# Reordering the seven Strassen block products of the FFN's second matrix in a two-layer decoder trunk

## The chip, the cores and the metric

The kernel runs on one core of a Trainium2 chip. The metric is the time of one execution on the device, in microseconds (us), smaller being better. Several executions were timed; one more was run under the hardware profiler, and everything said about engines, waits and transfers comes from that one.

## The reference

The program is a decoder trunk of two layers on 256 tokens of width 1024, all in float32. Each layer is a half-step feed-forward network (FFN), a mixer (a spatial gating branch beside differential attention) and a second half-step FFN, each followed by a residual sum and a layer norm. What the change touches is the second matrix of the FFN, `w2`, which stands four times in the program (two layers, two FFNs each):

```python
def _swiglu(x, w1, w3, w2):
    return (jax.nn.silu(x @ w1) * (x @ w3)) @ w2
...
    for l in range(DEPTH):
        h = _swiglu(x, ffn_w1[l, 0], ffn_w3[l, 0], ffn_w2[l, 0])
        x = _layernorm(ALPHA * x + 0.5 * h, ln_g[l, 0], ln_b[l, 0])
        h = _mixer(x, l, w_in[l], ...)
        x = _layernorm(ALPHA * x + h, ln_g[l, 1], ln_b[l, 1])
        h = _swiglu(x, ffn_w1[l, 1], ffn_w3[l, 1], ffn_w2[l, 1])
        x = _layernorm(ALPHA * x + 0.5 * h, ln_g[l, 2], ln_b[l, 2])
```

With h the 256 x 2816 hidden activation, `h @ w2` has 256 x 1024 outputs: two row tiles of 128 tokens by two column halves of 512.

## The kernel before

**Split operands.** A float32 operand is used as a sum of two parts that TensorE multiplies fast: a high part `whi`, copied by ScalarE (ACT), and a low part `wlo`, the difference, made by VectorE (DVE). A product takes three matmuls: high by high, low by high, high by low. Every weight therefore arrives by DMA as a raw tile, is split by one ACT and one DVE instruction for each piece of 128 x 1024, and is then used by TensorE (PE). `stream` does that for plain weights (its splits are lines 195 and 197), `pieces` for weights that take part in Strassen sums (both parts at lines 247 and 249, in `split`). There are eight buffers for high parts, eight for low parts (`HL`), and four for raw tiles (`RAW`).

**The w2 stage, `gemm_seven`.** The first 1024 of the 2816 rows of w2 are taken as a 2 x 2 block matrix w11, w12, w21, w22 (each 512 x 512), the first 1024 columns of h as a 2 x 2 matrix over the two row tiles, and their product is made by the Strassen-Winograd scheme with seven block products in place of eight. `product` issues one of them: 12 matmuls into one PSUM bank. The remaining rows of w2 are ordinary. For the first column half they come as seven pieces, and `between` takes one piece for both row tiles, which is again 12 matmuls. For the second column half `rest(1)` splits seven more pieces, which are held and used first for one row tile, then for the other (line 402).

So until `rest(1)` begins TensorE works through 14 slots of 12 matmuls, seven block products and seven pieces of `between`. They are counted here as slots 1 to 14. Before the change the order is: slot 1 w11 by block a11; 2 a piece; 3 w21; 4 a piece; 5 the sum r1 = w11 + w12 into the bank `bz`; 6 a piece; 7 the sum r1 + r3 (r3 is w22) into the bank `bx`; 8 a piece; 9 the plain block r3 into `bz`; 10 a piece; 11 r2 = w12 + w22 into `bx`; 12 a piece; 13 the last block product, r1 after w21 was added to it, into `bx`; 14 a piece.

**Sums on the way.** `plus` adds one raw tile to another on VectorE (line 356, two instructions of 128 x 1024). `gather` does the addition w21 into r1 by an accumulating DMA that GpSimd (POOL) issues in two halves (line 350); it may start once the splits of r1 + r3 have read r1. `ln.fold` (line 605, VectorE) adds the running content of `bx` or `bz` into the residual rows `xtok` in SBUF. TensorE goes on accumulating in the same bank, so the next product into that bank must wait until the fold has read it. There are five folds in each stage: after slot 1 (`bx`), after slot 5 (`bz`), after slot 7 (`bx`, the product with `sums[1]`), after slot 11 (`bx`) and after slot 13 (`bx`).

**What sets the order.** TensorE runs strictly in program order (a manual schedule). The other engines' orders are fixed when the program is built: a list scheduler takes what is ready in its own model of time, earlier program positions first, and each engine's queue then runs in that order on the chip. On top of that the `line` mechanism chains the high splits on ACT, and the low splits and `plus` additions on VectorE, in program order, from the start of the FFN's later part to the end of `rest(1)`. Folds are not in that chain, so where a fold stands between the splits is the scheduler's choice. Raw tiles are fetched by SP in one queue in the order of `step`.

**Timed side tasks.** `beside` tasks resume when a clock that `beat` advances by 1 for each 12 matmuls of this kind has gone far enough. `setup`, which runs once in the first FFN, waits 16 beats after its DMAs and then issues a few small VectorE instructions (lines 552 to 566) and one exponential on ACT (line 559).

Of the kernel before, what the change touches and what calls it, by code (L numbers as in the profile page):

```python
# [54 lines left out]
def trunk(ctx, tc, x, xT, w13a, w13b, w2, wb, wqk, wu, wg, wgr, wbr, wbrr, wo, gateb, gatebr, sgug, sgub, sguwT, sgubias, lam, diffg,  # L55
# [18 lines left out]
    def name(s):  # L74
        serial[0] += 1
        return f"{s}_{serial[0]}"

    def bank():
        return psum.tile([P, 512], F32, tag="main", name=name("bank"))

    def side_bank():
        return psum.tile([P, 512], F32, tag="side", name=name("sbank"))
# [18 lines left out]
    def s512(s, n=4):  # L101
        return tmp.tile([P, 512], F32, tag="side", name=name(s), bufs=n)
# [21 lines left out]
    def beat(w):  # L124

        clock[0] += w
        for task in list(tasks):
            if task[0] <= clock[0]:
                turn(task)
# [20 lines left out]
    def inline(eng, ins):  # L150
        if line[2]:
            line[eng is V] = ins
        return ins

    def behind(ins):

        return tc.issue_after(ins) if ins is not None else nullcontext()

    def fetch(src, width=CH, raw=None):

        step()
        if raw is None:
            raw = raw_pool.tile([P, CH], F32, tag="raw", name=name("raw"))
        for g in gate:
            g[0] -= 1
        while len(gate) > 1 and gate[1][0] < 0:
            gate.pop(0)
        with behind(gate[0][1] if gate and gate[0][0] < 0 else None):
            if isinstance(raw, list):
                for j, v in enumerate(raw):  # L170
                    loaded[0] = nc.sync.dma_start(v, src[:, j * HC : (j + 1) * HC]).ins
            else:
                loaded[0] = nc.sync.dma_start(raw[:, :width], src).ins
        return raw
# [70 lines left out]
    def split(hi, lo, src, eng=V, after=(None, None)):  # L245
        with behind(after[0]):
            a = A.activation(hi, src, AF.Copy).ins  # L247
        with behind(after[1]):
            return a, eng.tensor_tensor(out=lo, in0=src, in1=hi.bitcast(F32), op=ALU.subtract).ins  # L249
# [94 lines left out]
    def halved(v):  # L344
        return v if isinstance(v, list) else [v[:, o : o + HC] for o in range(0, CH, HC)]
# [7 lines left out]
    def plus(raw, more):  # L353
        for v, m in zip(halved(raw), halved(more)):
            with behind(line[1]):
                inline(V, V.tensor_tensor(out=v, in0=v, in1=m, op=ALU.add).ins)  # L356
        return raw

    def pieces(raw):
        out = []  # L360
        for v in halved(raw):
            hi = hi_pool.tile([P, HC], F32R, tag="hi", name=name("whi"))
            lo = lo_pool.tile([P, HC], F32R, tag="lo", name=name("wlo"))
            for eng, ins in zip((A, V), split(hi, lo, v, after=line[:2])):
                inline(eng, ins)
            out.append((hi, lo))
        return out

    def product(ps, x, w, start, stop):
        for k in range(4):  # L370
            hi, lo = (v[:, k % 2 * 512 : k % 2 * 512 + 512] for v in w[k // 2])
            for n, (y, o) in enumerate(((hi, 0), (lo, 0), (hi, 1))):
                PE.matmul(ps, x[o](k), y, start=start and k == n == 0, stop=stop and k == 3 and n == 2,  # L373
                          skip_group_check=True)
            beat(0.25)

    def gemm_seven(src, xh, xl, sums, spare, ln, done):

        q = [[bank(), bank()], [side_bank(), bank()]]
        bx, bz = side_bank(), q[1][0]
        (w11, w21), (w12, w22) = ([s[:, o : o + CH] for o in (0, CH)] for s in src)

        def rest(c):
            for k in range(8, FT, 4):
                nk = min(4, FT - k)
                for j, piece in enumerate(stream(src[c][:, k * 512 : (k + nk) * 512], nk * 512)):
                    yield k + 2 * j, piece

        def rows(t, c, k0, piece, o=0, n=512):
            for j in range(2):
                k = k0 + j
                hi, lo = (w[:, j * 512 + o : j * 512 + o + n] for w in piece)  # L400
                for m, (y, x) in enumerate(((hi, xh), (lo, xh), (hi, xl))):
                    PE.matmul(q[c][t][:, :n] if o == 0 else more[:, :n], x(k, t), y,  # L402
                              start=k == 8 and m == 0 and (c, t) != (1, 0), stop=k == FT - 1 and m == 2, skip_group_check=True)
            beat(n / 1024)

        def block(t, k0):
            return tuple(lambda k, f=f: f(k0 + k, t) for f in (xh, xl))

        a11, a12, a22 = block(0, 0), block(0, 4), block(1, 4)
        first = rest(0)  # L410

        def between():
            k, piece = next(first)
            for t in range(NT):
                rows(t, 0, k, piece)

        r1 = fetch(w11)
        p1 = pieces(r1)
        r2 = fetch(w12, raw=spare[0])
        plus(r1, r2)  # L420
        product(bx, a11, p1, True, False)
        ln.fold(0, 0, bx, ALU.add, True)
        between()
        product(q[0][0], a12, pieces(fetch(w21)), False, False)
        gather(r2, w22)
        r3 = fetch(w22, raw=spare[1])
        between()
        product(bz, sums[0], pieces(r1), True, False)
        ln.fold(1, 1, bz, ALU.add, True)
        between()  # L430
        product(bx, sums[1], pieces(plus(r1, r3)), False, False)
        ln.fold(0, 1, bx, ALU.subtract, True)
        gather(r1, w21)
        between()
        product(bz, sums[3], pieces(r3), False, False)
        between()
        product(bx, sums[2], pieces(r2), False, False)
        ln.fold(1, 1, bx, ALU.subtract, False)
        between()
        product(bx, a22, pieces(r1), False, True)  # L440
        ln.fold(1, 0, bx, ALU.add, True)
        between()
        for t in range(NT):
            done(t, q[0][t], 0, 512)
        held = list(rest(1))
        line[:] = None, None, False
        cuts = ((0, 512),), (((0, 256), (256, 256)) if ln.last else ((0, 512),))
        for t in range(NT):
            for o, n in cuts[t]:
                more = bank() if o else None  # L450
                for k, piece in held:
                    rows(t, 1, k, piece, o, n)
                done(t, (more if o else q[1][t])[:, :n], 512 + o, n)
# [85 lines left out]
    def setup(after):  # L539
        G.memset(mask[:, :P], 0.0)  # L540
        make_causal_mask(nc, mask[:, P:], NEG)
        lam_t = s512("lam").rearrange("p (l f d) -> p l f d", l=DEPTH, f=4)
        for dst, src in ((x_tok[0], x[:P, :]), (x_tok[1], x[P:, :]), (cos_t, cosT), (sin_t, sinT), (dgs, diffg),
                         (gbh, gateb), (ln_g, lngT), (ln_b, lnbT), (lam_t, lam.partition_broadcast(P))):
            first = dst
            while len(first.shape) > 2:
                first = first[:, 0]
            V.tensor_copy(first[:, :1], after)
            G.dma_start(dst, src)
        yield 16  # L550
        with behind(added[0]):
            V.tensor_scalar(out=gbh, in0=gbh, scalar1=0.5, scalar2=None, op0=ALU.mult)
        pr = s512("lampr").rearrange("p (l f d) -> p l f d", l=DEPTH, f=4)[:, :, :2]
        for j in range(2):
            with behind(added[0]):
                V.tensor_tensor(out=pr[:, :, j], in0=lam_t[:, :, 2 * j], in1=lam_t[:, :, 2 * j + 1], op=ALU.mult)
        ls = const.tile([P, DEPTH, 2], F32, name="ls")
        V.tensor_reduce(out=ls, in_=pr, op=ALU.add, axis=AX.X)
        A.activation(ls, ls, AF.Exp)
        for l in range(DEPTH):  # L560
            nl = const.tile([P, 1], F32, name=f"neg_lam{l}")
            V.tensor_scalar(out=nl, in0=ls[:, l, 1:2], scalar1=ls[:, l, 0:1], scalar2=-lambda_init(l),
                            op0=ALU.subtract, op1=ALU.add)
            neg_lam.append(nl)
            with behind(added[0]):
                V.tensor_scalar(out=dgs[:, l : l + 1], in0=dgs[:, l : l + 1], scalar1=1.0 - lambda_init(l),
                                scalar2=None, op0=ALU.mult)
# [757 lines left out]
```

## Time and profile before

| what | before |
|---|---|
| median of 3 runs | 1200.1 us |
| lowest and highest run | 1196.73 and 1202.01 us |
| the profiled execution, its own time | 1200.3 us |
| its span in the trace | 1198.5 us |
| mean granted TensorE clock | 0.999 |
| VectorE busy, share of the span | 1012.1 us, 84% |
| ACT busy, share of the span | 824.7 us, 69% |
| GpSimd busy, share of the span | 299.4 us, 25% |

Times inside the trace are counted from the start of the span. The four w2 stages have their 14 slots at about 124 to 167, 541 to 583, 720 to 758 and 1131 to 1171 us; they are called stages 1 to 4. A timeline row reads: start, duration, engine, line, operation, output and inputs, shape, count, and in brackets the idle time of the engine before it with what ended it. Rows of equal instructions that follow each other are merged, with their count behind the x.

### The profile page before, as it was taken

To read this page: it belongs to the slowest core of one execution; us is meant where nothing else is said; L and a number is where in the kernel's file an instruction comes from. 1 tells how busy PE (TensorE), PEld (TensorE's weight loads), DVE (VectorE), ACT (ScalarE), POOL (GpSimd) and SP (SyncE) were. 2 spreads that over 40 slices of the span, in tenths; PEclk is the share of its full clock that TensorE was granted. 3 is DMA by queue.
4 is the path that set the end of the run, shared out by engine and by line. 5 is a ranking of instruction groups with operands and counts; after the bars stand their busy time and mean duration, and the time that the engine had idled before them with its cause. 6 is when DMAs were issued, how large, how long until landed. Compare 5 with 4: busy or idle time off the path is not lost.

```text
span 1198.5 us, 16639 instructions
## 1 busy us (share of the span) xinstructions
PE 1183.9 (99%) x5771; PEld 993.0 (83%) x5771; DVE 1012.1 (84%) x1558; ACT 824.7 (69%) x1418; POOL 299.4 (25%) x356
## 2 busy tenths in 40 slices
PE   9999999999999999999999999999999999999998
PEld 7888778888888888887788888888888888888877
DVE  6889989888688989879899879888965989989795
ACT  6688658559955677885677886576788556679860
POOL 1112301137430220071020071003564112102500
PEclk9999999999999999999999999999999999999999
DMA  9969885757855758698668698676666754886870
GB/s 350 284 193 283 257 285 192 265 198 212 248 205 186 226 180 272 198 284 241 240 205 270 173 290 253 230 270 239 210 204 211 252 182 165 259 252 212 269 236 36
DMA packets 129220, 276.14 MB, mean 230 GB/s; under 512 B 89024, under 2 KB 90096, under 8 KB 104560
## 3 DMA queue, kind: packets, MB, share of 16 engines
q1 hardware_dynamic: 121392, 248.80, 62.3%
q0 software_dynamic: 7312, 25.76, 9.1%
q8 instruction: 45, 0.74, 0.2%
q10 hardware_dynamic: 432, 0.52, 0.1%
q14 instruction: 39, 0.32, 0.1%
HBM read 249.10 MB, written 1.05 MB: 209 GB/s over the span
## 4 chain that ended last, share of the span: by engine, by line
PE 84%; DMA 6%; DVE 5%; ACT 3%; issue 1%; POOL 0%; SPq 0%; ACTq 0%; DVEq 0%; POOLq 0%
PE bank L283 43%; PE bank L295 13%; PE sbank L373 8%; PE bank L302 7%; PE bank L402 6%; PE sbank L402 3%; DMA raw<-in_w 3%; DVE wlo L197 2%; PE bank L512 2%; PE sbank L984 1%; DMA spare<-in_w 1%; DVE wlo L249 1%; DMA planes<-planes 1%; ACT whi L195 1%; ACT whi L247 1%
## 5 line engine op out<-in xcount | busy, mean ns | idle before, releaser
L197 DVE TENSOR_TENSOR wlo<-raw,whi 128x1024 fp32r<-128x1024 f32 (+1 forms) x374 | 414.5, 1136 | 52.5 <-ACT whi L195 38.1
L195 ACT ACTIVATE whi<-raw 128x1024 fp32r<-128x1024 f32 (+1 forms) x378 | 351.8, 959 | 135.1 <-PE bank L283 43.7
L283 PE MATMUL bank<-whi,x 128*128 128x512 f32 x1224 | 386.3, 390 | 0.0
L283 PEld LDWEIGHTS bank<-whi,x 128*128 128x128 f32 x1224 | 229.8, 188 | 47.8
L283 PE MATMUL bank<-wlo,x 128*128 128x512 f32 x612 | 238.2, 389 | 0.0
L295 PE MATMUL bank<-x,whi 128*128 128x512 f32 x640 | 153.3, 391 | 0.0
L295 PEld LDWEIGHTS bank<-x,whi 128*128 128x128 f32 x640 | 118.2, 188 | 23.8
L283 PEld LDWEIGHTS bank<-wlo,x 128*128 128x128 f32 x612 | 114.9, 188 | 23.2
L247 ACT ACTIVATE whi<-raw 128x1024 fp32r<-128x1024 f32 (+1 forms) x96 | 92.4, 983 | 60.2 <-DVE raw L356 35.1
L249 DVE TENSOR_TENSOR wlo<-raw,whi 128x1024 fp32r<-128x1024 f32 (+1 forms) x96 | 110.1, 1161 | 12.5 <-ACT whi L247 12.3
L229 POOL COPY seven<-seven 128x512 uint16<-128x512 uint16 x16 | 67.1, 4253 | 105.9 <-ACT whi L195 54.5
L302 PEld LDWEIGHTS bank<-x,wlo 128*128 128x128 f32 x640 | 81.4, 191 | 2.9
L302 PE MATMUL bank<-x,wlo 128*128 128x256 f32 x640 | 82.6, 283 | 0.0
L402 PE MATMUL bank<-whi,hhi 128*128 128x512 f32 (+1 forms) x182 | 68.3, 375 | 0.8 <-DVE silu L305 0.8
L402 PE MATMUL bank<-whi,hlo 128*128 128x512 f32 (+1 forms) x182 | 67.9, 373 | 0.0
L402 PE MATMUL bank<-wlo,hhi 128*128 128x512 f32 (+1 forms) x182 | 67.9, 373 | 0.0
L960 POOL TENSOR_TENSOR swap<-swap,sin_t 128x512 f32<-128x512 f32 x16 | 25.9, 1618 | 103.4 <-DMA swap<-z 59.3
L719 POOL COPY nvia<-ntwo 128x256 uint16<-128x256 uint16 x20 | 9.9, 539 | 159.1 <-DMA ntwo<-nvia 108.0
L303 ACT ACTIVATE r<-bank 128x256 f32<-128x256 f32 x96 | 34.0, 372 | 12.9 <-PE bank L302 12.8
L373 PE MATMUL sbank<-whi,xhs 128*128 128x512 f32 x128 | 42.0, 389 | 0.0
L402 PEld LDWEIGHTS bank<-whi,hhi 128*128 128x128 f32 x182 | 34.3, 188 | 7.2 <-DVE silu L305 1.3
L402 PEld LDWEIGHTS bank<-whi,hlo 128*128 128x128 f32 x182 | 34.3, 188 | 6.1
(286 smaller groups left out, 2159.1 us busy)
## 6 DMA issues: line engine op xcount, KB each, us to landing
raw<-in_w13b SPq DMA_DIRECT2D x68, 1024.0 KB, 5.5
raw<-in_w SPq DMA_DIRECT2D x32, 1024.0 KB, 6.4
raw<-in_wb SPq DMA_DIRECT2D x16, 1024.0 KB, 5.5
raw<-in_wqk SPq DMA_DIRECT2D x16, 1024.0 KB, 5.7
r<-in_w13b SPq DMA_DIRECT2D x16, 512.0 KB, 5.9
raw<-in_w13a SPq DMA_DIRECT2D x8, 1024.0 KB, 4.8
raw<-in_wgr SPq DMA_DIRECT2D x8, 1024.0 KB, 5.4
raw<-in_wg SPq DMA_DIRECT2D x8, 1024.0 KB, 5.1
```

The lines of the kernel that those rows point to most:

```text
L195: inline(A, A.activation(h, r, AF.Copy).ins)
L197: low = eng.tensor_tensor(out=w, in0=r, in1=h.bitcast(F32), op=ALU.subtract).ins
L229: eng.tensor_copy(out=o, in_=i)
L247: a = A.activation(hi, src, AF.Copy).ins
L249: return a, eng.tensor_tensor(out=lo, in0=src, in1=hi.bitcast(F32), op=ALU.subtract).ins
L283: PE.matmul(ps, xx, w, start=start and n == 0, stop=stop and n == 2)
L295: PE.matmul(b[-1], hi[:, k * P : (k + 1) * P], xc(k), start=k == 0, stop=False)
L302: PE.matmul(b[n][:, :T], lo[:, k * P : (k + 1) * P], xc(k)[:, :T], start=False, stop=k == KT - 1)
L303: emptied[0] = A.activation(r[:, s], b[n][:, T:], AF.Copy, scale=scale).ins
L373: PE.matmul(ps, x[o](k), y, start=start and k == n == 0, stop=stop and k == 3 and n == 2, skip_group_check=True)
L402: PE.matmul(q[c][t][:, :n] if o == 0 else more[:, :n], x(k, t), y, start=k == 8 and m == 0 and (c, t) != (1, 0), stop=k == FT - 1 and m == ...
L960: turned_by[0] = G.tensor_tensor(out=s3, in0=s3, in1=s, op=ALU.mult).ins
```

## The change

The plain block product of r3 moves from slot 9 to slot 7, the summed block r1 + r3 with its fold and its gather moves from slot 7 to slot 9, and the last block product moves from slot 13 to slot 14, behind the seventh piece of `between`. The new order is: 5 r1 into `bz`, 6 a piece, 7 r3 into `bz`, 8 a piece, 9 r1 + r3 into `bx`, 10 a piece, 11 r2 into `bx`, 12 and 13 two pieces, 14 the last block product into `bx`. No instruction is added or taken away. In `setup` the wait grows from 16 to 22 beats.

```diff
         product(bz, sums[0], pieces(r1), True, False)
         ln.fold(1, 1, bz, ALU.add, True)
         between()
+        product(bz, sums[3], pieces(r3), False, False)
+        between()
         product(bx, sums[1], pieces(plus(r1, r3)), False, False)
         ln.fold(0, 1, bx, ALU.subtract, True)
         gather(r1, w21)
         between()
-        product(bz, sums[3], pieces(r3), False, False)
-        between()
         product(bx, sums[2], pieces(r2), False, False)
         ln.fold(1, 1, bx, ALU.subtract, False)
         between()
+        between()
         product(bx, a22, pieces(r1), False, True)
         ln.fold(1, 0, bx, ALU.add, True)
-        between()
         for t in range(NT):
             done(t, q[0][t], 0, 512)
...
-        yield 16
+        yield 22
         with behind(added[0]):
             V.tensor_scalar(out=gbh, in0=gbh, scalar1=0.5, scalar2=None, op0=ALU.mult)
```

## The prediction

> **What bounds the kernel now.** I read the engines' totals on the page first, then what TensorE waited for, then the four w2 stages one by one.
>
> ```profile
> PE 1183.9 (99%) x5771; PEld 993.0 (83%) x5771; DVE 1012.1 (84%) x1558; ACT 824.7 (69%) x1418; POOL 299.4 (25%) x356
> ```
>
> TensorE shows 1183.9 of 1198.5 us, so a reordering that leaves all 5771 matmuls in place can only win back waits: 14.6 us in the whole program. The next view cuts out the 14 slots of each stage, from the first matmul of slot 1 to the first of `rest(1)`; the columns are length, then busy time of each engine with its count.
>
> ```profile
> core 0: us, PE busy (x) PEld busy (x) DVE busy (x) ACT busy (x) POOL busy (x), PEclk, DMA share, GB/s
> 124.50:167.16 42.66, 39.23 (x171) 31.31 (x169) 38.84 (x52) 26.88 (x36) 6.35 (x7) 1.00 0.85 288
> 540.57:582.69 42.12, 39.33 (x170) 31.23 (x169) 40.06 (x47) 24.89 (x32) 3.70 (x5) 1.00 0.84 260
> 719.60:757.81 38.21, 38.21 (x170) 31.47 (x169) 37.61 (x45) 24.19 (x31) 2.94 (x5) 1.00 0.91 291
> 1131.12:1170.74 39.62, 38.82 (x170) 31.31 (x169) 37.69 (x46) 25.59 (x34) 2.88 (x5) 1.00 0.73 225
> ```
>
> Stage 3 runs without a wait: 38.21 us, 2.73 for each slot. It is the floor. The others stand over it by 4.45, 3.91 and 1.41, together 9.8 us, the most that the change can touch. VectorE is nearly a second bound: 37.61 of 38.21 us in stage 3. Which waits make up the excess, in the list of TensorE's waits:
>
> ```profile
> PE sbank L373 <- DVE xtok L605: 3.4, 3, 1.4
> PE sbank L373 <- ACT whi L247: 1.3, 1, 1.3
> PE sbank L373 <- DVE wlo L249: 1.2, 2, 0.8
> PE bank L402 <- DVE silu L305: 0.8, 1, 0.8
> ```
>
> The same waits in TensorE's timeline, two rows of stage 1, two of stage 2, one of stage 4:
>
> ```profile
> 142.26 0.50 PE L373 MATMUL sbank<-whi,sum 128*128 128x512 f32 x1 [1.25 <-ACT whi L247]
> ...
> 558.95 0.50 PE L373 MATMUL sbank<-wlo,sum 128*128 128x512 f32 x1 [0.47 <-DVE wlo L249]
> ...
> 161.63 0.47 PE L373 MATMUL sbank<-whi,hhi 128*128 128x512 f32 x1 [1.34 <-DVE xtok L605]
> ...
> 577.16 0.47 PE L373 MATMUL sbank<-whi,hhi 128*128 128x512 f32 x1 [1.41 <-DVE xtok L605]
> ...
> 1165.22 0.47 PE L373 MATMUL sbank<-whi,hhi 128*128 128x512 f32 x1 [0.61 <-DVE xtok L605]
> ```
>
> So there are two places. Slot 7 waits for the splits of the summed block (two additions and then the splits, all on a full VectorE). Slot 13 waits for the fold of slot 11. A matmul is shown 0.39 us long while the next one starts 0.23 after it, so an idle time understates its loss by 0.16: slot 13 costs 1.50, 1.57 and 0.77 in stages 1, 2 and 4. The rest of the excess is slot 7's: 4.45 - 1.50 = 2.95 in stage 1; in stage 2, after 1.0 for the `silu` wait in slot 2, which the change does not touch, 3.91 - 1.57 - 1.0, about 1.2 to 1.3 (I take 1.2); in stage 4 a slot of 2.88 us for 2.72, 0.16.
>
> **The last product behind two pieces.** Stage 2 on VectorE, from the splits of slot 6's fetch (line 197) on:
>
> ```profile
> 552.99 2.35 DVE L197 TENSOR_TENSOR wlo<-raw,whi 128x1024 fp32r<-128x1024 f32 x2
> 555.26 2.35 DVE L356 TENSOR_TENSOR raw<-raw,spare 128x1024 f32<-128x1024 f32 x2
> 557.67 1.23 DVE L249 TENSOR_TENSOR wlo<-raw,whi 128x1024 fp32r<-128x1024 f32 x1
> 558.81 0.68 DVE L605 SCALAR_TENSOR_TENSOR xtok<-xtok,sbank 128x512 f32<-128x512 f32 x1
> 559.41 1.22 DVE L249 TENSOR_TENSOR wlo<-raw,whi 128x1024 fp32r<-128x1024 f32 x1
> 560.54 2.35 DVE L249 TENSOR_TENSOR wlo<-spare,whi 128x1024 fp32r<-128x1024 f32 x2
> 562.82 1.22 DVE L197 TENSOR_TENSOR wlo<-raw,whi 128x1024 fp32r<-128x1024 f32 x1
> 563.95 0.68 DVE L605 SCALAR_TENSOR_TENSOR xtok<-xtok,sbank 128x512 f32<-128x512 f32 x1
> ...
> 570.65 1.23 DVE L249 TENSOR_TENSOR wlo<-raw,whi 128x1024 fp32r<-128x1024 f32 x1 [1.22 <-ACT whi L247]
> 571.79 4.63 DVE L197 TENSOR_TENSOR wlo<-raw,whi 128x1024 fp32r<-128x1024 f32 x4
> 576.33 0.68 DVE L605 SCALAR_TENSOR_TENSOR xtok<-xtok,sbank 128x512 f32<-128x512 f32 x1
> ```
>
> Each addition or split takes 1.135 us (2.27 from row to row for two), a fold 0.6. The fold of slot 11 comes at 576.33, behind the last splits of r1 and four later pieces, because those r1 splits had waited for the gather: VectorE stood 1.22 us. With slot 14 for the product in place of slot 13 TensorE has one more piece, 2.72 us, to spend, against waits of 1.50, 1.57 and 0.77. The seventh piece's split also passes ahead of the gather's wait on both engines. I take all three waits as gone: **3.84 us**. What it costs: the fold of slot 13, covered by a piece before, now lies beside `rest(1)`, which writes other banks; without that cover it would cost its 0.68 in each stage. The gather itself, two transfers on GpSimd's queue, starts 2.27 us later, behind the splits of r3, and its product stands 2.72 later; nothing else on GpSimd changes place, and SP's fetches keep their order.
>
> **The plain block at slot 7.** Its splits need no additions: r3 is in SBUF before slot 7 in every stage, since the additions that read it already ran at 555.26 without idle time before them, and so in the rows of the other stages below (if it lands only just then, ACT's high split of 1.06 us comes on top). So the split that TensorE wants at slot 7 comes 2.27 us earlier than now, which is more than stage 2's 1.2 us and most of stage 1's 2.95. But the product goes into `bz`, and `bz` must first be folded. Before, this fold (the row at 558.81) had slots 6, 7 and 8 as its cover. Now it has slot 6 alone, so **where it stands in VectorE's queue sets the wait**. The trace of before cannot show the new order. It shows the old: behind five instructions counted from the first split of slot 6's fetch (two splits, two additions, one split). The scheduler places a fold when its model of TensorE reaches the end of slot 5, and nothing ahead of that moves. So I take five again: two splits, the two splits of r3, one addition. The fold then ends 3 x 1.135 + 0.68 = 4.08 us after the row that now begins the additions. Stage 2: 555.26 + 4.08 = 559.34. The other stages have these rows:
>
> ```profile
> 139.85 2.35 DVE L356 TENSOR_TENSOR raw<-raw,spare 128x1024 f32<-128x1024 f32 x2
> 143.39 0.68 DVE L605 SCALAR_TENSOR_TENSOR xtok<-xtok,sbank 128x512 f32<-128x512 f32 x1
> ...
> 731.92 2.35 DVE L356 TENSOR_TENSOR raw<-raw,spare 128x1024 f32<-128x1024 f32 x2
> 735.46 0.68 DVE L605 SCALAR_TENSOR_TENSOR xtok<-xtok,sbank 128x512 f32<-128x512 f32 x1
> ...
> 1143.65 2.36 DVE L356 TENSOR_TENSOR raw<-raw,spare 128x1024 f32<-128x1024 f32 x2
> ```
>
> This gives 143.93, 736.00 and 1147.73. When TensorE wants slot 7 is read from the last matmul of slot 6 in stage 1 and the first of slot 7 in the others:
>
> ```profile
> 140.62 0.39 PE L402 MATMUL bank<-whi,hlo 128*128 128x512 f32 x1
> 558.09 0.39 PE L373 MATMUL sbank<-whi,sum 128*128 128x512 f32 x1
> 735.95 0.39 PE L373 MATMUL sbank<-whi,sum 128*128 128x512 f32 x1
> 1147.96 0.39 PE L373 MATMUL sbank<-whi,sum 128*128 128x512 f32 x1
> ```
>
> The waits at slot 7 become 143.93 - 140.85 = 3.1, then 1.25, 0.05 and 0. Against 2.95, 1.2, 0 and 0.16 now, this place gives nothing: **-0.1 us** in all. Its bounds: each instruction that the fold moves forward wins up to 1.135 in stages 1 and 2 (2.3 for the first, then 1.2 and less), each that it moves back costs that in every stage (4.3 for the first, with 0.9 in stage 4, then 4.5).
>
> **The summed block at slot 9.** Additions and splits now have slots 7 and 8 as cover. Taking stage 2: the first split of r1 + r3 ends near 555.26 + 5 x 1.135 + 0.6 = 561.5, slot 9 is wanted at 558.09 + 1.25 + 5.44 = 564.8; no wait. Its fold has one piece as cover in place of three slots, and slot 11 waits for it; by the same count of time it falls about nine instructions after the first fold, 0.6 + 8 x 1.135 + 0.6 later, at 568.9 to 569.5, with slot 11 wanted at 570.2. I take zero; it can cost (second rival).
>
> **The later `setup`.** A few instructions of at most 0.48 us on VectorE and one table load on ACT change place within stage 1. In the worst case they still stand ahead of slot 7, as now; in the best they free VectorE there. I take zero, and up to 1 us of gain for the range.
>
> **The sum.** 3.84 - 0.1 = 3.7 us less, against the profiled execution's own 1200.3: 1196.6. That execution stands 0.2 over the median of the runs, so I say **1196.5 us**.
>
> **The rivals.**
>
> *All the waits go.* The fold of `bz` is placed one or two instructions earlier. Then slot 7 costs 2.0 or 0.8 in stage 1, 0.1 or 0 in stage 2, and the gain is 6.0 to 7.6, with the `setup` instructions out of the way up to 8.3: 1192 to 1194.3, say 1193. For it speaks that on the chip slot 5 is over by 735.95 - 2.72 = 733.2 in stage 3, 2.2 us ahead of the fold at 735.46; against it that the order is fixed at build time, when the old count was five.
>
> *The gain is given back at slot 11.* The fold of the summed block lands behind the first split of the last r1, which waits for the gather. How long that takes, in rows of GpSimd and ACT from stage 2 and stage 3:
>
> ```profile
> 559.20 0.89 POOL L350 DMA_DIRECT2D raw<-in_w  x1 [5.01 <-DVE wlo L249]
> 567.11 1.06 ACT L247 ACTIVATE whi<-raw 128x1024 fp32r<-128x1024 f32 x1 [2.63 <-DMA raw<-in_w]
> ...
> 737.58 0.86 POOL L350 DMA_DIRECT2D raw<-in_w  x1 [0.86 <-DVE wlo L249]
> 743.81 1.06 ACT L247 ACTIVATE whi<-raw 128x1024 fp32r<-128x1024 f32 x1 [1.45 <-DMA raw<-in_w]
> ```
>
> 7.9 us in stage 2, 6.2 in stage 3. Issued at 561.6 it would land at 569.5; ACT split 1.06, VectorE split 1.14, fold 0.68: 572.4 for a slot wanted at 570.2, 2.2 us. Stage 1 alike, a little less; stages 3 and 4 would stay near zero. About 3.5 us: 1200. The same time comes out if the fold of `bz` falls one instruction later. For it: the count above puts this fold just at that edge.
>
> *Slower: the bz fold behind the summed block.* If the model puts the fold behind the second addition and both splits of r1 + r3, it ends 7.5 us after the addition row: slot 7 waits 6.5, 4.7, 3.5 and 3.2 us, which is 13.5 more than in the forecast and leaves the kernel 9.8 slower: 1210. After the second addition alone the gain is already used up; with one split too it is 1205. For it: before, the fold did stand behind both additions and a split of that block; against it, that those now come two instructions later. The Trainium skill (TensorE: Matmul & The Clock Gate, the table in "Why this matters for your kernels") warns of idle times over about 3 us, after which the matmul clock is halved for a while. No row here shows it: PEclk is 1.00 in all four windows, whose waits stay under 1.5 us. By that rule an estimate for this rival is some 1.7 us more for each such wait, near 1216.
>
> **How the numbers follow.** The forecast has 0.36, with its own range 1194.5 to 1198.5; all waits gone 0.26; given back 0.20; slower 0.18. The measurement of this kernel tells about 0.5%, 6 us, from no change. Faster than 1194.1: the first rival nearly whole and the edge of the forecast, 0.30. Slower than 1206.1: most of the last, 0.16. Within: 0.54. The range goes from 1191, below the first rival, to 1205.5, which takes in the first two steps of the slow one.
>
> **What would show it.** The idle rows ending at line 605 ahead of the last product are gone; what remains at slot 7 is named line 605 and not a split, some 3 us in stage 1 and 1.2 in stage 2; the four windows read about 41.3, 40.6, 38.3 and 38.7 us. A fold row of `bz` behind two splits of `spare` and one addition proves the count. It is wrong if the idle time stands ahead of slot 11, if stage 3 grows, or if the time won in the windows is missing at the end, as it would be if the stages behind are bound by transfers.

## The result, and the profile after

| what | before | after |
|---|---|---|
| median of 17 runs each, same chip | 1200.1 us | 1204.98 us |
| lowest and highest run | 1196.45 and 1202.85 us | 1200.39 and 1210.83 us |
| the profiled execution, its own time | 1200.3 us | 1208.93 us |
| its span in the trace | 1198.5 us | 1206.9 us |

The ratio is 1.0042, with a 95% interval of 1.0025 to 1.0059: the change makes the kernel about 5 us slower, where 3.7 us of gain had been forecast. A second series of the same kernel, shown below, gave 1.0030 (1.0005 to 1.0054).

TensorE issues the same 5771 matmuls. The four windows of 14 slots, as in the prediction (length, then busy time of each engine, then PEclk):

```profile
124.94:171.52 46.58, 41.18 (x171) 33.54 (x169) 38.12 (x52) 26.37 (x36) 5.44 (x7) 0.93 0.79 261
544.92:585.76 40.84, 38.76 (x171) 31.29 (x169) 37.43 (x44) 22.39 (x29) 3.69 (x5) 1.00 0.80 249
722.62:761.94 39.32, 38.70 (x170) 31.33 (x169) 35.35 (x42) 21.14 (x28) 2.87 (x5) 1.00 0.83 258
1135.25:1179.59 44.34, 38.98 (x171) 31.25 (x169) 39.50 (x48) 27.17 (x35) 3.69 (x5) 1.00 0.65 202
```

The forecast was about 41.3, 40.6, 38.3 and 38.7. Together they are 8.47 us longer than before (171.08 against 162.61), which is the whole difference of the spans, 8.4. So nothing of the loss lies outside the stages. TensorE's waits in them, first by what ended them, then the rows of the timeline:

```profile
PE sbank L373 <- DVE xtok L605: 9.0, 4, 5.4
PE bank L402 <- DVE silu L305: 2.9, 2, 2.5
...
PE bank L373 <- DVE bc L571: 1.5, 1, 1.5
```

```profile
146.85 0.77 PE L373 MATMUL sbank<-whi,sum 128*128 128x512 f32 x1 [5.40 <-DVE xtok L605]
...
563.81 0.47 PE L373 MATMUL sbank<-whi,sum 128*128 128x512 f32 x1 [1.68 <-DVE xtok L605]
...
759.13 0.47 PE L373 MATMUL sbank<-whi,hhi 128*128 128x512 f32 x1 [0.62 <-DVE xtok L605]
...
1140.68 0.50 PE L402 MATMUL bank<-whi,hhi 128*128 128x512 f32 x1 [2.52 <-DVE silu L305]
...
1146.78 0.50 PE L373 MATMUL bank<-wlo,hhi 128*128 128x512 f32 x1 [1.50 <-DVE bc L571]
...
1168.62 0.47 PE L373 MATMUL sbank<-whi,sum 128*128 128x512 f32 x1 [1.34 <-DVE xtok L605]
```

The first two rows are slot 7 of stages 1 and 2, the third is the last product, now slot 14, of stage 3, the last is slot 11 of stage 4. All four wait for a fold. The two rows between, in slots 2 and 3 of stage 4, are of another kind: they come ahead of every product that the change moves. The losses in slots 1 to 5 made 1.8 us in the profile of before, 5.4 in this one, 2.6 in a second profile of the very same kernel (which is 2.9 of the 3.5 us between these two executions), and between 2.9 and 11.6 in the other kernels below. Why they scatter is not known; with one profile of before, and it the lowest, a part of the order in them is not excluded. They are left out of what follows. The losses in slots 6 to 14 are the ones to compare, a loss being the time from the first matmul of a slot to that of the next, less the 2.72 us of the floor. Each row is one profile, and two profiles of one kernel differ by up to 1.5 us in a stage. Each ratio is taken against the kernel before as timed in the same series. For every kernel profiled, in us:

| kernel | stage 1 | 2 | 3 | 4 | sum | ratio to before, 95% interval |
|---|---|---|---|---|---|---|
| before | 4.5 | 2.8 | 0.1 | 1.0 | 8.5 | 1 |
| after | 8.5 | 2.0 | 1.2 | 1.6 | 13.3 | 1.0042 (1.0025 to 1.0059) |
| after, second series (e5) | 8.2 | 3.6 | 0.8 | 0.8 | 13.3 | 1.0030 (1.0005 to 1.0054) |
| new order, setup at 16 (e1) | 5.5 | 0.9 | 2.7 | 0.8 | 9.9 | 1.0011 (0.9987 to 1.0035) |
| the same, second series (e12) | 4.9 | 1.5 | 2.0 | 0.7 | 9.1 | 1.0020 (0.9993 to 1.0046) |
| swap of slots 7 and 9 alone (e2) | 7.5 | 9.4 | 8.7 | 7.3 | 32.9 | 1.0237 (1.0201 to 1.0273) |
| last product alone (e3) | 0.7 | 1.1 | 1.1 | 0.8 | 3.6 | 0.9982 (0.9961 to 1.0003) |
| the same, second series (e10) | 1.8 | 0.7 | 1.2 | 1.0 | 4.7 | 0.9980 (0.9960 to 1.0000) |
| setup at 22 alone (e7) | 7.2 | 2.2 | 0.2 | 1.4 | 10.9 | 1.0008 (0.9984 to 1.0032) |
| new order in stages 2 to 4 only (e4) | 4.7 | 3.3 | 0.4 | 0.9 | 9.3 | 1.0008 (0.9992 to 1.0025) |
| after, r3's splits behind h (e6) | 6.6 | 2.8 | 2.7 | 0.6 | 12.7 | 1.0007 (0.9983 to 1.0031) |
| bz and slot 9 folds first (e8) | 4.7 | 3.7 | 6.9 | 1.3 | 16.6 | 1.0023 (0.9997 to 1.0050) |
| bz and slot 11 folds first, setup 16 (e9) | 2.6 | 0.0 | 0.5 | 0.0 | 3.1 | 0.9978 (0.9959 to 0.9997) |
| the same, setup 22 (e13) | 6.7 | 0.5 | 0.0 | 0.0 | 7.2 | 1.0002 (0.9979 to 1.0024) |
| the same, setup 12 (e14) | 0.3 | 0.5 | 0.5 | 0.0 | 1.3 | 0.9961 (0.9936 to 0.9986) |
| last product alone, setup 12 (e11) | 0.0 | 1.2 | 0.5 | 0.0 | 1.6 | 0.9963 (0.9943 to 0.9982) |
| the same, second series (e15) | 0.0 | 1.2 | 1.1 | 0.5 | 2.8 | 0.9955 (0.9934 to 0.9976) |

**Stage 1: why slot 7 waits 5.4 us.** ACT and VectorE of the kernel after, up to the fold that TensorE waits for:

```profile
138.02 1.06 ACT L247 ACTIVATE whi<-spare 128x1024 fp32r<-128x1024 f32 x1 [4.55 <-DMA spare<-in_w]
138.99 0.61 ACT L247 ACTIVATE hhi<-planes 128x512 fp32r<-128x512 f32 x1
...
139.63 0.69 DVE L249 TENSOR_TENSOR hlo<-planes,hhi 128x512 fp32r<-128x512 f32 x1 [4.12 <-ACT hhi L247]
...
141.44 0.17 DVE L552 TENSOR_SCALAR gbh<-gbh 128x32 f32<-128x32 f32 x1
...
142.05 0.42 DVE L558 TENSOR_REDUCE ls<-lampr 128x4 f32<-128x256 f32 x1
142.38 2.35 DVE L249 TENSOR_TENSOR wlo<-spare,whi 128x1024 fp32r<-128x1024 f32 x2
144.65 0.33 DVE L562 TENSOR_SCALAR neg_lam<-ls 128x1 f32<-128x1 f32 x2
144.89 1.22 DVE L356 TENSOR_TENSOR raw<-raw,spare 128x1024 f32<-128x1024 f32 x1
146.03 0.68 DVE L605 SCALAR_TENSOR_TENSOR xtok<-xtok,sbank 128x512 f32<-128x512 f32 x1
```

Read it from below. The fold at 146.03 stands behind two splits of `spare` and one addition, exactly the count that was forecast, but 2.8 us late (its end was forecast for 143.93, and is 146.71). Of that, 0.4 is the later start of the whole stage (124.94 for 124.50), and some 1.2 us are `setup`: from 141.44 to 142.38, and 0.24 at 144.65. The rest comes from above: VectorE stood 4.12 us for the last high split of h, `hhi<-planes`, which ACT could not begin because the instruction ahead of it in its queue, r3's high split, itself stood 4.55 us for r3's transfer. r3 is in SBUF in time for slot 7, and not in time for its new place in ACT's queue.

**The clock.** After the 5.40 us the matmuls run slower. Two windows behind that wait:

```profile
147.00:149.50 2.50, 2.50 (x6) 1.97 (x7) 2.45 (x3) 2.10 (x3) 0.22 (x1) 0.50 0.03 8
149.50:152.00 2.50, 2.50 (x7) 1.97 (x6) 2.50 (x3) 2.50 (x4) 1.54 (x2) 0.50 0.47 59
```

The granted clock, 1.00 in all windows of before, is 0.50 here: six or seven matmuls in 2.5 us in place of eleven. By the starts of the slots that costs 2.5 us in slot 7 and 0.4 in slot 8.

**Stages 2 to 4.** The fold of `bz` in stage 2, and in stage 4 the gather's second half on GpSimd, r1's first split on both engines and the fold that slot 11 waits for:

```profile
559.57 2.36 DVE L249 TENSOR_TENSOR wlo<-spare,whi 128x1024 fp32r<-128x1024 f32 x2 [0.32 <-ACT whi L247]
561.85 1.22 DVE L356 TENSOR_TENSOR raw<-raw,spare 128x1024 f32<-128x1024 f32 x1
562.98 0.68 DVE L605 SCALAR_TENSOR_TENSOR xtok<-xtok,sbank 128x512 f32<-128x512 f32 x1
...
1159.84 0.87 POOL L350 DMA_DIRECT2D raw<-in_w  x1 [0.40 <-DVE wlo L249]
...
1165.57 1.06 ACT L247 ACTIVATE whi<-raw 128x1024 fp32r<-128x1024 f32 x1 [2.54 <-DMA raw<-in_w]
...
1166.66 1.23 DVE L249 TENSOR_TENSOR wlo<-raw,whi 128x1024 fp32r<-128x1024 f32 x1 [1.44 <-ACT whi L247]
1167.80 0.68 DVE L605 SCALAR_TENSOR_TENSOR xtok<-xtok,sbank 128x512 f32<-128x512 f32 x1
...
1169.05 1.06 ACT L247 ACTIVATE whi<-raw 128x1024 fp32r<-128x1024 f32 x1 [2.42 <-DMA raw<-in_w]
```

The first three rows show the forecast's place again. The others show the place that the second rival named: the fold of the summed block stands behind the first split of the last r1, which waits for the gather. The second half lands by 1169.05, 9.2 us after its issue at 1159.84. Before, the second half took 8.5, 8.6, 6.2 and 7.8 us from issue to its split; in this kernel 9.0, at most 8.9, 9.9 and 9.2, and 9.1 to 10.9 in the second series.

### The profile page after: what moved, and what is told of

It is laid out like the page before. It is cut to its first block, busy times and chain, and to the rows that moved or that the text cites. A ratio compares the mean times of both kernels' runs of the same rounds, so it can differ in the third digit from the quotient of the medians.

```text
span 1206.9 us, 16650 instructions
## 1 busy us (share of the span) xinstructions
PE 1186.2 (98%) x5771; PEld 995.5 (82%) x5771; DVE 1012.0 (84%) x1558; ACT 824.1 (68%) x1418; POOL 296.6 (25%) x356
## 4 chain that ended last, share of the span: by engine, by line
PE 87%; DMA 5%; DVE 5%; ACT 1%; issue 1%; SPq 0%; ACTq 0%; DVEq 0%
PE bank L283 45%; PE bank L295 13%; PE sbank L373 9%; PE bank L302 7%; PE bank L402 5%; DMA spare<-in_w 3%; PE sbank L402 3%; PE bank L512 2%; DVE wlo L249 1%; DMA raw<-in_w 1%; DVE wlo L197 1%; PE sbank L984 1%; DVE raw L356 1%; PE sbank L1040 1%; PE sbank L1158 1%
## 5 line engine op out<-in xcount | busy, mean ns | idle before, releaser
L373 PE MATMUL sbank<-whi,sum 128*128 128x512 f32 x96 | 33.9, 416 | 8.4 <-DVE xtok L605 8.4
```

## The experiments

Each is an edit of the kernel after or before; all ratios are in the table above.

**Setup left alone (e1, e12).** The kernel after with

```diff
-        yield 22
+        yield 16
```

> The new order of the seven products in all four stages, with the wait in setup back at 16 beats. Theory A (in stage 1 the high split of r3 stands in ACT's queue, waiting for its transfer, ahead of a split of h that VectorE needs first): the idle time ahead of slot 7 in stage 1 stays between 4 and 5.5 us, and the time falls only by the 1.2 us that the setup instructions now take on VectorE between slot 6's splits and the fold: 1203 to 1205, ratio to the kernel before 1.002 to 1.005. Theory C (the later setup instructions are the cause): the wait falls under 3 us and the time to 1200 or less, ratio under 1.000.

> The whole new order with the setup left at 16 beats, a second time. Theory (the later setup costs 2 to 4 us in stage 1 in this order, because r3's high split then stands ahead of the last high split of h on ACT; the rest of the change about breaks even): no block of ACT and VectorE ahead of slot 7 of stage 1, ratio 0.999 to 1.002, below the changed kernel's 1.0042 and 1.0030. Rival (the setup's place is worth nothing and the first ratio, 1.0011, was chance): ratio 1.003 to 1.005.

Ratios 1.0011 and 1.0020. In e1 the wait is 3.39 us, outside the bounds of both theories. Stage 1 of the second series, on ACT, VectorE and TensorE:

```profile
136.50 0.62 ACT L247 ACTIVATE hhi<-planes 128x512 fp32r<-128x512 f32 x1
137.24 2.01 ACT L247 ACTIVATE whi<-spare 128x1024 fp32r<-128x1024 f32 x2
...
137.56 0.33 DVE L562 TENSOR_SCALAR neg_lam<-ls 128x1 f32<-128x1 f32 x2
...
137.87 0.68 DVE L249 TENSOR_TENSOR hlo<-planes,hhi 128x512 fp32r<-128x512 f32 x1
...
143.07 0.68 DVE L605 SCALAR_TENSOR_TENSOR xtok<-xtok,sbank 128x512 f32<-128x512 f32 x1
...
143.90 0.77 PE L373 MATMUL sbank<-whi,sum 128*128 128x512 f32 x1 [3.24 <-DVE xtok L605]
```

h's split now stands ahead of r3's, nothing waits for r3, the last instruction of `setup` is done ahead of h's last low split, and the fold ends at 143.75, 0.2 us from the forecast for stage 1; the wait is 3.24 for 3.1. Stage 1 loses 3.0 and 3.6 us less than in the kernel after. The difference of the ratios is of the same sort, about 0.2%, but the intervals overlap. The rest of the change shows no gain either: both intervals take in 1.

**The swap alone (e2).** As e1, and the last product back in slot 13:

```diff
         between()
-        between()
         product(bx, a22, pieces(r1), False, True)
         ln.fold(1, 0, bx, ALU.add, True)
+        between()
```

> Only r3's product and the summed block change places (slots 7 and 9); the last product stays in slot 13 and setup at 16 beats. Theory A: stage 1's window is 4 to 6 us longer than before, stage 2 about as before, stages 3 and 4 within 1.5 us of it; the time 1203 to 1206. Theory B (the fold of bz, which now has one piece as its cover, costs in every stage): each of the four windows longer by 1 us or more.

1232.84 us, by far the slowest. Stage 3, GpSimd, ACT, VectorE and TensorE:

```profile
757.03 0.86 POOL L350 DMA_DIRECT2D raw<-in_w  x1 [0.41 <-DVE wlo L249]
...
766.59 1.06 ACT L247 ACTIVATE whi<-raw 128x1024 fp32r<-128x1024 f32 x1 [3.89 <-DMA raw<-in_w]
...
767.68 1.23 DVE L249 TENSOR_TENSOR wlo<-raw,whi 128x1024 fp32r<-128x1024 f32 x1 [3.72 <-ACT whi L247]
768.82 0.68 DVE L605 SCALAR_TENSOR_TENSOR xtok<-xtok,sbank 128x512 f32<-128x512 f32 x1
...
769.65 0.77 PE L373 MATMUL sbank<-whi,sum 128*128 128x512 f32 x1 [5.16 <-ACT whi L195]
```

Both theories missed what happened. Here the fold of slot 9 stands behind both splits of the last r1, and slot 11 waits 5.0 to 5.3 us for the gather in every stage. (The last row names a split on ACT that ended at about the same time as the fold; the splits of slot 11's own weight, r2, had ended by 761.3.) Neither piece of slot 10 nor any other work covers that, and the half clock after each wait takes about 2 us more. The prediction's second rival, the fold of the summed block behind a split that waits for the gather, is real. In e1, which differs from this kernel by the last product's move alone, slots 10 to 14 lose 2.7 us in all four stages in place of 29.7: the move puts r1's splits further back and keeps most of it away.

**The last product alone (e3, e10).** The kernel before, with only this:

```diff
         between()
+        between()
         product(bx, a22, pieces(r1), False, True)
         ln.fold(1, 0, bx, ALU.add, True)
-        between()
```

> Only the last product moves behind the seventh piece (slot 14); slots 7 and 9 and setup as before. If this half of the change is worth what was forecast: the waits ahead of the last product of 1.50, 1.57 and 0.77 us are gone, the time falls by 3 to 4 us to 1196 to 1197, ratio 0.997. If the gain is given back later, the first halves of the stages are shorter and the time is 1199 to 1201.

> The old order with the last block product alone moved behind the seventh piece, a second time. Theory (this part earns what the prediction gave it, 3.84 us in the profiled execution of before): no wait at slots 11 to 14, ratio 0.996 to 0.999. Rival (the first ratio, 0.9982 with an interval that reached 1.0003, was chance, and the stages behind take back what the windows win): ratio 0.999 to 1.002.

Ratios 0.9982 and 0.9980. The four windows of the first:

```profile
124.85:165.28 40.43, 38.99 (x171) 31.31 (x170) 37.89 (x50) 24.01 (x33) 5.70 (x7) 1.00 0.93 297
538.70:579.62 40.92, 39.07 (x170) 31.31 (x169) 38.36 (x45) 23.27 (x31) 4.28 (x6) 1.00 0.85 264
716.53:757.09 40.56, 39.08 (x171) 31.30 (x169) 39.22 (x47) 24.48 (x32) 3.67 (x5) 1.00 0.86 272
1130.39:1169.80 39.41, 39.01 (x170) 31.31 (x169) 37.60 (x47) 25.72 (x34) 2.93 (x5) 1.00 0.74 227
```

161.32 us together, 1.3 less than before although slots 1 to 5 lost 3.6 more; slots 6 to 14 lose 4.9 less. (1.6 of the 3.6 stand in stage 1, ahead of everything that the edit moves.) No wait is left at slots 11 to 14 in any stage of either run. The ratios are worth 2.2 and 2.4 us, and their intervals reach 1.0003 and 1.0000.

**Setup at 22 in the old order (e7).** The kernel before with `yield 22`.

> The kernel before with the wait in setup at 22 beats and nothing else. Theory A: there is no early split of r3 here, so no blocked ACT queue; ratio to the kernel before 0.999 to 1.001. Theory C: as much slower as the changed kernel loses by it, 1.002 to 1.003.

Ratio 1.0008. The profile has the small instructions ahead of slot 7's additions: TensorE's first wait at slot 7 of stage 1 is 2.27 us in place of 1.25, the granted clock halves behind it, and stage 1 loses 2.6 us more than before; the ratio does not resolve it. ACT is not blocked here, since r3's split stands later in the old order. The small instructions cost time by themselves; for the block the new order is needed as well.

**The new order in stages 2 to 4 only (e4).** The kernel after with `yield 16` and a parameter that keeps the old order in the first FFN:

```diff
-        product(bz, sums[3], pieces(r3), False, False)
-        between()
+        if early:
+            product(bz, sums[3], pieces(r3), False, False)
+            between()
...
+        if not early:
+            product(bz, sums[3], pieces(r3), False, False)
+            between()
...
-        between()
+        if early:
+            between()
         product(bx, a22, pieces(r1), False, True)
         ln.fold(1, 0, bx, ALU.add, True)
+        if not early:
+            between()
```

> The new order in the second, third and fourth stage, the old one in the first; setup at 16 beats. Theory A: the loss was stage 1's, so this is 4 us under the changed kernel or more, 1198 to 1200.5, ratio 0.998 to 1.000. Theory B: three quarters of the loss stay, 1203 to 1204, ratio 1.003.

Ratio 1.0008, between the two theories: the order without stage 1 neither wins nor loses measurably; stages 2 to 4 lose 4.6 us in slots 6 to 14, against 4.0 before.

**The changed kernel again (e5).** 

> The changed kernel itself once more, as the measure for the two kernels beside it, and as a second trace of it. If the placing of the queues explains the loss, the order of instructions is the same and the idle time ahead of slot 7 in stage 1 is again over 4 us; the waits that depend on when a transfer lands (slots 2, 11, 14) come out differently. Ratio to the kernel before 1.002 to 1.006.

Ratio 1.0030, and the same wait of 5.51 us at slot 7 of stage 1.

**r3's splits behind h's last split (e6).** The kernel after, with setup at 22, and the following, where `split_of_h[0]` is the latest high split of h on ACT:

```diff
-        product(bz, sums[3], pieces(r3), False, False)
+        with behind(split_of_h[0]):
+            p3 = pieces(r3)
+        product(bz, sums[3], p3, False, False)
```

> The changed kernel, setup still at 22 beats, with one edge of order added: the high splits of r3 stand behind the last split of h in ACT's queue. Theory A (r3's split waits on ACT for its transfer ahead of the split of h, and VectorE waits for that one): VectorE's 4.1 us of idle time in stage 1 goes, slot 7's loss there falls from 8 to 4 or 5 us, and the time by about 3 us against the changed kernel. Theory C (the setup instructions' own time on VectorE and the table load are the cost): the loss falls by less than 1 us.

Ratio 1.0007. The 4.12 us of VectorE are gone and the fold comes 1.06 us earlier (144.97), but slot 7 still waits 3.77 us, and slots 6 to 8 of stage 1 lose 6.6 us in place of 8.2 to 8.5, more than theory A allowed. `setup` still lies in front, and an earlier fetch landed late in this run: ACT has it at 132.67, 8.3 us after slot 1's first matmul, for 7.0 in e12. In e1 it was 8.2, and there, with `setup` at 16 beats, the wait was 3.39 and the slots lost 5.3. The time falls by 2.8 us against e5 in the same series (1.0007 for 1.0030), about theory A's figure, but the intervals overlap.

**The folds put ahead (e8, e9).** Both are the kernel after with setup at 16 and the additions of r1 + r3 queued behind the fold of `bz`. In e8 the last r1's splits are queued behind the fold of slot 9, in e9 behind that of slot 11. e9:

```diff
-        ln.fold(1, 1, bz, ALU.add, True)
+        bz_read = ln.fold(1, 1, bz, ALU.add, True)
...
-        product(bx, sums[1], pieces(plus(r1, r3)), False, False)
+        with behind(bz_read):
+            plus(r1, r3)
+        product(bx, sums[1], pieces(r1), False, False)
...
-        ln.fold(1, 1, bx, ALU.subtract, False)
+        bx_read = ln.fold(1, 1, bx, ALU.subtract, False)
...
-        product(bx, a22, pieces(r1), False, True)
+        with behind(bx_read):
+            p1 = pieces(r1)
+        product(bx, a22, p1, False, True)
```

> The new order with setup at 16 beats and two edges of order: the additions r1 + r3 stand behind the fold of bz, and the splits of the last r1 behind the fold of the summed block. If the folds' places in VectorE's queue are what took the gain in stages 2 to 4, the waits at line 605 ahead of slots 7, 11 and 14 are gone there (under 0.3 us each), stage 1 keeps 2 to 4 us at slot 7, and the time is 1197 to 1199 where the kernel before has 1201 to 1202, ratio 0.996 to 0.998. If the gain was lost to transfers that land later, the waits stay, ratio 1.000 or more.

> The changed order with the setup at 16 beats, with the additions of r1 + r3 queued behind the fold of bz, and the splits of the last r1 (the one that waits for the gather) queued behind the fold of slot 11, so that both folds of bx pass ahead of the instructions that wait for the gather. Theory (the change loses because folds stand in VectorE's queue behind a split that waits for a transfer): no wait of TensorE at slot 11 nor at slot 14 in any stage, what is left stands at slot 7 (2 to 4 us in stage 1, 1.1, 0.2 and 0 in stages 2 to 4), about 4.5 us over the floor of 2.72 us a slot in all beside the waits at slots 1 to 3, which vary; ratio to the kernel before 0.996 to 0.998. Rival (the gather lands too late whatever stands in the queue): a wait at slot 14 named after a split of r1 takes the place of the fold's, 1 to 3 us in most stages, ratio 1.000 or more.

e8 got no faster (1.0023): the waits at slot 11 were gone, and the next fold, that of slot 11, stood behind the splits that wait for the gather, so that slot 14 waited 2.10 and 3.70 us in stages 2 and 3. e9 gave 0.9978. Its stage 3 on VectorE and ACT, and its window of stage 2:

```profile
743.84 0.68 DVE L609 SCALAR_TENSOR_TENSOR xtok<-xtok,sbank 128x512 f32<-128x512 f32 x1
747.67 0.69 DVE L609 SCALAR_TENSOR_TENSOR xtok<-xtok,sbank 128x512 f32<-128x512 f32 x1 [3.16 <-PE sbank L373]
...
748.23 1.06 ACT L247 ACTIVATE whi<-raw 128x1024 fp32r<-128x1024 f32 x1 [3.96 <-DMA raw<-in_w]
```

```profile
539.55:577.65 38.10, 38.10 (x170) 31.54 (x169) 34.26 (x42) 23.23 (x31) 3.07 (x5) 1.00 0.80 246
```

The gather lands as late as ever, 9.7 us after its issue, and ACT stands 3.96 us for it; but both folds (line 609 in this kernel) have passed, the second of them waiting for TensorE and not the other way round. Stage 2 runs on the floor. So the gather itself is not too late; what hurts is a fold that stands behind it. Of the 6.0 us that slots 6 to 14 lose less than in e12, 4.4 lie in slots 6 and 7, where the fold of `bz` is one instruction earlier and stage 1 no longer falls to the half clock (its wait is 2.02 us), and 1.6 in slots 10 to 14.

**The same with other places of setup (e13, e14), and the last product alone with setup at 12 (e11, e15).** e9 with `yield 22` and with `yield 12`; e3 with `yield 12`.

> The changed order and the changed setup, both whole, with only the two folds put ahead (the additions of r1 + r3 behind the fold of bz, the last splits of r1 behind the fold of slot 11). Theory (the two causes are separate and add up): stage 1 shows the block of ACT behind r3's fetch again and loses 5 to 8 us at slots 6 to 8, stages 2 to 4 lose nothing at slots 6 to 14; ratio 1.000 to 1.002, that is 2 to 5 us over the same kernel with the setup at 16 (0.9978). Rival (the folds alone made the loss, the setup's part is taken up by waits that come anyway): stage 1 loses 2 to 3 us at slots 6 and 7, ratio 0.997 to 0.999.

> The changed order with the two folds put ahead and the setup at 12 beats. Theory (the setup's instructions cost time at slots 6 to 8 of stage 1 wherever VectorE is the bound, and none four beats earlier): the wait at slot 7 of stage 1 falls from 2.0 us to 1 or less, no waits at slots 11 and 14 in any stage, ratio 0.995 to 0.998. Rival (what is left at slot 7 of stage 1 is the fold of bz alone, whatever the setup does): 2 us there as before, ratio 0.997 to 0.999.

> The old order with the last block product behind the seventh piece, and the setup at 12 beats in place of 16. Theory (in stage 1 the setup's small VectorE instructions and its exponential take time at slots 6 to 8, where VectorE is the bound; four beats earlier they lie in the part ahead of slot 1): the loss at slots 6 and 7 of stage 1 falls by about 1 us against the same order with the setup at 16, ratio 0.995 to 0.998. Rival (their place does not matter in the old order): the same loss at slots 6 and 7, ratio as with the setup at 16, 0.997 to 1.000, or they only take the time from the part ahead.

> The old order with the last block product behind the seventh piece and the setup at 12 beats, a second time. Theory (it is the fastest of the versions tried): stage 1 at the floor of 38.2 us or within 1 us of it at slots 6 to 14, ratio 0.995 to 0.998. Rival (the first ratio, 0.9963, was partly chance): 0.998 to 1.000.

With 22 the block is back, on VectorE and TensorE of e13:

```profile
139.40 0.69 DVE L249 TENSOR_TENSOR hlo<-planes,hhi 128x512 fp32r<-128x512 f32 x1 [2.04 <-ACT hhi L247]
...
144.66 0.68 DVE L609 SCALAR_TENSOR_TENSOR xtok<-xtok,sbank 128x512 f32<-128x512 f32 x1
...
145.49 0.76 PE L373 MATMUL sbank<-whi,sum 128*128 128x512 f32 x1 [4.47 <-DVE xtok L609]
```

Stage 1 loses 6.7 us in place of e9's 2.6, and the ratio goes from 0.9978 to 1.0002; slots 11 and 14 stay free of waits. The two causes are separate. With setup at 12 stage 1 has next to nothing left to win; the first window of e14 and of e11:

```profile
124.06:162.42 38.36, 38.36 (x171) 31.39 (x169) 32.89 (x39) 23.41 (x31) 10.36 (x12) 1.00 0.85 254
```

```profile
124.29:162.40 38.11, 38.11 (x170) 31.54 (x169) 35.72 (x43) 26.07 (x34) 8.97 (x11) 1.00 0.98 321
```

The order on ACT does not cost by itself: in e14 r3's first high split stands ahead of the last two high splits of h, but its transfer has landed at 134.40, 10.6 us after its issue (138.02 and 13.4 us in the kernel after), and slot 7 does not wait. Why it lands earlier there is not shown.

The ratios are 0.9961 for e14 and 0.9963 and 0.9955 for the old order with the last product behind two pieces (e11, e15). Both versions beat the kernel before, and with it the kernel after; their intervals do not tell them apart: the new order of the blocks, put right, is worth no more than the old order with one line moved and an earlier `setup`.

## Why the prediction was wrong

**The last product behind two pieces: right, and given back in part.** The three waits, priced at 3.84 us, are gone in e3 and e10, whose slots 6 to 14 lose 4.9 and 3.9 us less (the rest is slot 7's scatter); the ratios are worth 2.3, with intervals that take in 3.84. In the changed kernel the three waits are gone too, but stage 3 has a new one of 0.62 at slot 14, and the second series one of 1.24 in stage 2. The step that was too short is "its product stands 2.72 later", with the gather's own time left as it was: in stage 3 the gather's second half goes out at 742.81 against 737.58 before, 2.2 us later counted from slot 1, as forecast (2.27), but it then takes 9.9 us in place of 6.2.

**The plain block at slot 7: the place of the fold was right, the time nearly right for stages 2 to 4.** The fold stood behind two splits and one addition in every stage. Its waits were forecast at 3.1, 1.25, 0.05 and 0 and read 5.40, 1.68, 0 and 0; with setup at 16 stage 1 read 3.24 and 3.39. That stage 3 came out at 0 is in part luck: there e1, e6 and e12 read 1.21, 1.24 and 1.20, each in a run in which slot 2 of that stage had waited 1.1 to 1.6 us. "This place gives nothing" held without the later `setup`, apart from the clock and stage 3. (In the first rival, the fold two places earlier, the gain of 7.6 is by the prediction's own terms 7.3.)

**The later setup: the step that failed.** It was put at zero because "in the worst case they still stand ahead of slot 7, as now". They do, and that is not harmless: with 16 beats they had run by 138.0 in VectorE's timeline (e12), ahead of the chain that ends in the fold, and now they lie in it. In the new order the later beat also goes with r3's first high split ahead of h's last one on ACT. The prediction asked only whether r3 was in SBUF before slot 7, not what is queued behind the instruction that waits for it. Cost: stage 1 loses 2.7 to 3.6 us more in slots 6 to 14 with 22 beats than with 16 (8.5 and 8.2 against 5.5 and 4.9), 4.1 with the folds ahead (e13 against e9). The rows divide it roughly. The wait at slot 7 is 2.0 to 2.3 us longer. 1.2 of that is the small instructions' own time. About 1.0 is the block of ACT: VectorE begins h's last low split 1.6 to 1.8 us ahead of the beginning of TensorE's wait at slot 7 in after, e5 and e13, where r3's split stands ahead, and 2.6 to 2.9 in e1, e9 and e12. The remaining 0.8 to 1.4 is the longer stretch of half clock. In the ratios the later `setup` is 0.0020 (the mean of after and e5 against that of e1 and e12) and 0.0024 (e13 against e9). Neither pair resolves it by itself. It would be about half of the 5 us.

**The clock: read as a rule that no row showed, and it decided 2.9 us.** The prediction applied it to its slowest rival alone. Its own forecast for stage 1, 3.1 us, was long enough for it: after 3.24 the kernel of e12 lost 1.5 us in slot 7, after 5.40 the kernel after lost 2.9 in slots 7 and 8. The Trainium skill (TensorE: Matmul & The Clock Gate, "Part 1: The HAM clock gate") has the clock fall to one half after an idle window of about 3.4 us and run full again after a busy one. The trace agrees in kind: PEclk 0.50, for some 6 us after the wait of 5.40; but the clock fell after shorter waits too (3.24 here, 2.01 in the last section). The estimate of 1.7 us for each such wait was too low for this one and a little too high for e12's.

**The summed block at slot 9: zero was wrong, and the second rival's place came true.** Its fold stands behind the first split of the last r1; that costs 1.5 us at slot 11 of stage 4 here and 0.2 to 0.4 in three stages of the second series. The rival had put 3.5 us on it, in stages 1 and 2; the size and the stages depend on when the gather lands.

**The sum.** For slots 6 to 14 the forecast leaves 4.4 us of loss, all at slot 7. The kernel after has 13.3: 8.5 at slots 6 to 8 of stage 1 for 3.1 forecast, 2.0 in stage 2 for 1.25, 0.3 in stage 3 for 0.05, 1.5 at slot 11 and 0.8 at slot 14 for zero. Against 8.5 before that is 4.8 more, which agrees with the medians' 4.9. The later `setup` is not all of it: without it (e1, e12) the slots still lose 9.9 and 9.1, since the half clock behind stage 1's wait (1.5 us), slot 7 of stage 3 (1.4) and slots 10 to 14 (2.7 and 2.0) had each been put at next to nothing. "It is wrong if the idle time stands ahead of slot 11, if stage 3 grows" named two of these, and not the largest, which stood at slot 7 of stage 1.

What stays open: whether the division of stage 1's loss between the block of ACT and the small instructions holds (it is read from single profiles, and e6 gives the block a larger share), and why the waits in slots 1 to 5 scatter so much.

## What to carry to other kernels

When an instruction that waits for a transfer moves forward in an in-order queue, ask not only whether its data are there when its consumer wants them, but what stands behind it in that queue until they are. A read that frees an accumulator, such as a fold, should be tied ahead of additions and splits that its consumer does not need, above all of a split that waits for a transfer; here two such edges took the ratio from 1.0020 to 0.9978, most of it, by the profiles, through a fold put ahead of one addition. Test the parts of a change one by one: one moved line and an earlier `setup` were worth 0.4%, and the swap of the two blocks with a later `setup` cost more than the moved line had won.

## What was not expected of the hardware

In the four stages of these runs the granted clock fell to 0.50 during or just after every wait of TensorE of 2.7 us and more (14 of them), five of the eleven between 2.0 and 2.6 us, and none of the ten between 1.5 and 2.0. After 2.52 us (row 1140.68 above) it stayed at 1.00, while in stage 4 of e10 a wait of 2.01 us in slot 2 (at 1132.49) was followed by this stretch, 0.60 in its mean:

```profile
1135.00:1138.00 3.00, 3.00 (x9) 2.33 (x9) 2.88 (x6) 2.99 (x7) 0.00 (x0) 0.60 1.00 403
```

So a wait under 2 us cost itself alone, and a longer one up to some 3 us on top of itself (2.9 in the kernel after). The second surprise is the accumulating transfer. Stage 3 from its second half's issue to r1's second split, before and after:

```profile
737.58:743.80 6.22, 6.22 (x29) 5.15 (x28) 6.22 (x7) 4.62 (x5) 0.86 (x1) 1.00 0.98 183
```

```profile
742.81:752.60 9.79, 9.79 (x44) 7.96 (x44) 7.11 (x7) 4.24 (x5) 0.86 (x1) 1.00 1.00 266
```

The same transfer took 6.2 us in the one place and 9.8 in the other, with the DMA engines full in both (share 0.98 and 1.00) but 266 GB/s moved beside it in place of 183. That the fetches of SP running beside it are what stretches it fits these rows; no run took them away.
